# Four groups of the second layer's modulation run at the end of the first layer's experts instead of inside its attention stage

## The chip, the cores and the metric

The program runs on one core of one Trainium2 chip. The metric is the device time of one execution in microseconds (us). The core's engines are PE (TensorE matmuls), PEld (its weight loads), DVE (VectorE), ACT (ScalarE), POOL (GpSimd) and SP (SyncE, which here issues almost all DMAs); each runs its own instructions in order and waits on semaphores for the others. A name such as L297 is a line of the kernel.

## The reference

Two layers of a diffusion transformer over 512 latent and 256 context tokens of width 1024, in f32. What matters here, cut from the reference:

```
m_lat = split(c_act @ w_mod[layer] + b_mod[layer], 6)          # w_mod[layer]: 1024 x 6144
m_ctx = split(c_ctx_act @ w_mod[layer] + b_mod[layer], 6)
h  = rmsnorm(x,  norm1_g[layer]) * (1 + m_lat[1]) + m_lat[0]
hc = rmsnorm(xc, norm1_g[layer]) * (1 + m_ctx[1]) + m_ctx[0]
p = h @ w_in[layer];  pc = hc @ w_in[layer]                     # then four mixers, one of them MLA, one HGRN
x = x + m_lat[2] * (concat(mixers) @ w_out[layer])
h2 = rmsnorm(x, norm2_g[layer]) * (1 + m_lat[4]) + m_lat[3]
x = x + m_lat[5] * hierarchical_moe(h2)                         # 32 experts, top 2 of one group
```

In the first layer the context tokens go through the same steps. The modulation is a product with two rows (c_act and c_ctx_act), but a matrix of 24 MB for each layer. It depends on c and c_ctx alone, not on the tokens.

## The kernel before

**Modulation.** `modulation(L, gs, slot, bank)` (L322) works in groups of 512 of the 6144 columns. For a group it loads the bias (two small DMAs, L332) into one of four tiles `bmt` and the weights in two DMAs of 1 MB (L337), does 64 matmuls whose two useful rows come from `cT` (L338), adds the bias on DVE (`mr`, L341) and, for groups 0 to 3, transposes (L343) and copies the result into `ABs[L]` (L344, L349). Groups 0 to 3 are m[0] and m[1]: they are what `htmp`, the modulated tokens at the very start of a layer (L505), needs. `drain` runs a generator to its end; `weave` runs several side by side, each with a number of steps.

**Stages of a layer.** Norm and projection w_in with the first mixer's work; GLA and neighbourhood attention; then the stage that matters here, in which HGRN, MLA and `mods()` (L1431) are woven (L1436, `STEPS[L][6]` to `[8]`); then the output projection, the routing and the experts. In the first layer `mods()` does groups 4 to 11 of this layer and behind them groups 0 to 3 of the next. In the second layer it does groups 4 to 11 alone.

**Experts.** Their weights (three 1 MB pieces of each of 32) stream through 18 slots (`wslot`), loaded by SP far ahead (`prefetch`). `pair(p_)` is two experts; 16 pairs run one after another, each ending in a scatter of `yes` into `XA` in DRAM by POOL (L2013). A pair may have more tokens than its tile holds, for which there are branches (L2038 and on), and behind the loop stands a branch for what is left over (L2052, `If(cregs[NP] > 64)`). It isn't taken with these inputs. At its untaken side every engine passes an unconditional branch with waits.

**Start of the next layer.** `fetch` loads 128 tokens from `XA` (`xn<-XA`, L473); ACT squares and sums (`junk`, L481), and `rstd_of` takes Ln (L300) and Exp (L301); DVE scales `xn` (L487); PE transposes it (L498); ACT makes `htmp` (L505). `wchunk` loads a piece of w_in (L522), which ACT and DVE split into two parts (L527, L531): the first piece is small (128 columns), and behind its split, which a call `fixed` ties in the order, comes a load of an activation table that holds both Ln and Exp (`ln_exp`, L191). A scheduler orders the instructions of each engine by costs and dependences; an activation that needs a table that isn't in place gets a load of its own.

Of the kernel before, what the change touches and what calls it, by code (L numbers as in the profile page):

```python
# [17 lines left out]
P = 128  # L18
# [7 lines left out]
NEXP = 32  # L26
# [7 lines left out]
YE = 3  # L34
PRE = 2

STEPS = ((38, 24, 60, 18, 12, 12, 66, 72, 12), (38, 24, 60, 18, 12, 12, 66, 72, 8))
NWM = 4
NU, NX, NM = 25, 8, 8
TOKS = ((256, 512), (0, 256))  # L40
# [45 lines left out]
def hybrid_kernel(ctx: ExitStack, tc: tile.TileContext, a: dict, out: bass.AP, dbg=None, stop=None):  # L86
    nc = tc.nc
# [235 lines left out]
    for t_ in bmt:  # L323
        V.memset(t_, 0.0)

    def modulation(L, gs, slot=None, bank=None):

        for i_, g in enumerate(gs):
            cs = slice(g * 512, (g + 1) * 512)
            bt = bmt[i_ % 4]  # L330
            for w in range(2):
                nc.sync.dma_start(bt.rearrange("(j r) c -> j r c", r=32)[:, w, :], a["b_mod"][L, cs].rearrange("(j c) -> j c", j=4))  # L332
            pm = bank()[:, 0:P] if bank else pmd()
            for k in range(KT):
                if k % 4 == 0:
                    wt = (slot or ring)([P, 4, 512])
                    nc.sync.dma_start(wt, a["w_mod"][L, k * P:(k + 4) * P, cs].rearrange("(k p) c -> p k c", p=P))  # L337
                for j in range(4):  # L338
                    mm(pm[32 * j:32 * j + 32, 0:P], cT[:, k, :], wt[:, k % 4, j * P:(j + 1) * P], k == 0, k == KT - 1)
            mr = cp.tile([P, P], F32, name="mr", tag="mr", bufs=2)  # L340
            V.tensor_tensor(mr, pm[:, 0:P], bt, op=ALU.add)  # L341
            if g < 4:
                TE.transpose(pm[:, 0:P], mr, ident)  # L343
                V.tensor_copy(ABs[L][:, :, g // 2, 4 * (g % 2):4 * (g % 2) + 4],  # L344
                              pm[:, 0:P].rearrange("p (j c) -> p c j", j=4)[:, 0:2, :])
            if g in (2, 3):
                ks = slice(4 * g - 8, 4 * g - 4)
                for w in range(2):
                    V.scalar_tensor_tensor(ABs[L][:, w, 1, ks], ABs[L][:, w, 1, ks], 1.0, g1s[:, L, ks], op0=ALU.add, op1=ALU.mult)  # L349
            if g in (8, 9):  # L350
                g2 = cp.tile([P, P], F32, name="g2", tag="g2", bufs=1)
                V.memset(g2, 0.0)
                for w in range(2):
                    nc.sync.dma_start(g2.rearrange("(j r) c -> j r c", r=32)[:, w, :],
                                      a["norm2_g"][L, (g - 8) * 512:(g - 7) * 512].rearrange("(j c) -> j c", j=4))
                V.scalar_tensor_tensor(mr, mr, 1.0, g2, op0=ALU.add, op1=ALU.mult)
            if 6 <= g < 10:
                TE.transpose(pm[:, 0:P], mr, ident)
                V.tensor_copy(AB2s[L][:, :, g // 2 - 3, 4 * (g % 2):4 * (g % 2) + 4],
                              pm[:, 0:P].rearrange("p (j c) -> p c j", j=4)[:, 0:2, :])  # L360
            if g >= 4:
                if g in (6, 7):

                    V.tensor_copy(bt.rearrange("p (e q) -> p q e", e=2), mr.rearrange("p (q e) -> p q e", e=2))
                for w in range(2):
                    if g in (6, 7):
                        nc.sync.dma_start(MOD[L][w, 3 * D:4 * D].rearrange("(e i j q) -> i j e q", e=2, i=2, j=4)[g - 6],
                                          bt.rearrange("(j r) (e q) -> j r e q", r=32, e=2)[:, w])
                    else:
                        nc.sync.dma_start(MOD[L][w, cs].rearrange("(j c) -> j c", j=4),  # L370
                                          mr.rearrange("(j r) c -> j r c", r=32)[:, w, :])
            yield
# [18 lines left out]
    def layer(L):  # L391
        last = L == DEPTH - 1
# [1037 lines left out]

        def mods():  # L1431
            yield from modulation(L, range(4, 12))
            if not last:
                yield from modulation(L + 1, range(4))

        weave((hgrn_, st[6]),  # L1436
              (chain(mla_qkv(Em, hu, cs, c2, mw, mr_), restore(Ex), mla(Em, mr_)), st[7]), (mods(), st[8]))
# [15 lines left out]
        def wslot():  # L1453
            i = pieces[0] % NW
            pieces[0] += 1
            for p_, n_ in slots:
                if i < n_:
                    return wpools[p_].tile([P, 2048], F32, name=f"w{p_}", tag=f"w{p_}", bufs=n_)
                i -= n_
# [21 lines left out]
        def prefetch(n, order=True, after=None, deep=DEEP):  # L1481

            for _ in range(n):
                e, i = len(loaded) // 6 + NEXP // 2 * (len(loaded) % 2), len(loaded) % 6 // 2
                if len(loaded) < 3 * NEXP:
                    loaded.append(expert_part(wgu[e], wdn[e], i, order, after, deep))
# [432 lines left out]
        def block_in(xg, xT=None, engs=(S.copy, V.tensor_copy)):  # L1919
# [8 lines left out]
                engs[g](xT[:, 4 * g:4 * g + 4], pt.rearrange("p (k t) -> p k t", k=4))  # L1928
            return xT

        def span(hv):
            return slice(64 * hv[0], 64 * hv[-1] + 64)

# [33 lines left out]
        def gates_of(own):  # L1967

            if last:
                return gate[:, 0]  # L1970
            gt = gts[:, 0]
            G.tensor_scalar(gt, gate[:, 1], own, None, op0=ALU.mult)
            G.tensor_tensor(gt, gt, gate[:, 0], op=ALU.add)
            return gt
# [35 lines left out]
        def scatter(ye, row):  # L2010


            G.indirect_dma_start(out=XA, out_offset=bass.IndirectOffsetOnAxis(ap=row, axis=0), in_=ye, in_offset=None,  # L2013
                                 bounds_check=T - 1, oob_is_err=False, compute_op=ALU.add)
# [3 lines left out]
        def pair(p_):  # L2018
            return [loaded[6 * p_ + h:6 * p_ + 6:2] for h in range(2)] if p_ >= 0 else None
# [5 lines left out]
        xT = block_in(xgs[0], None, (S.copy, S.copy))  # L2025
        for p_ in range(NP):
            prefetch(max(0, min(6 * p_ + NW, 3 * NEXP) - len(loaded)), False)
            w_ = pair(p_)
            xT_, ac = xT, block_up(w_, xT)
            if p_ == 0:  # L2030
                slot_weights(ohs, tabs[0])
                slot_weights(slot_table(wk, 1, tabs[1]["row"]), tabs[1])
            rows(p_ + NG)
            if p_ + 1 < NP:
                xT = into(p_ + 1)
            gt = gates_of(tab(0, p_, "own"))
            ye = weighted(p_, block_down(w_, block_act(ac)), gt, tab(0, p_, "gws"))
            with tc.If(cregs[p_] > 0):  # L2038
                with tc.If(cregs[p_] < 2) as c1_:
                    half_swapped(p_, w_[0], xT_, ye, gt, 1)  # L2040
                with c1_.Else():
                    with tc.If(cregs[p_] < 3) as c2_:
                        half_swapped(p_, w_[1], xT_, ye, gt, 0)
                    with c2_.Else():
                        swapped(p_, w_, xT_, ye, gt)

                        gather(yes[:, (p_ + 2) % YE], tab(1, p_, "row"))
                        y1 = block_down(w_, block_act(block_up(w_, into(p_, 1, xT_))))
                        scatter(weighted(p_ + 1, y1, gates_of(tab(1, p_, "own")), tab(1, p_, "gws")), tab(1, p_, "row"))
            scatter(ye, tab(0, p_, "row"))  # L2050

        with tc.If(cregs[NP] > 64):  # L2052
            for b in range(2, 12):
                t_ = tables(wk, "g")
                slot_weights(slot_table(wk, b, t_["row"]), t_)
                for i_, n_ in enumerate(kinds):
                    nc.sync.dma_start(TBL[:, :, (b - 2) * nk + i_].rearrange("a p -> p a"),
                                      t_[n_] if n_ == "row" else t_[n_].bitcast(I32))
            pieces[0] = 6
            with tc.For_i(0, NP) as e:  # L2060
                w_ = [[expert_part(wgu[bass.ds(e + NP * h, 1)].rearrange("o k c -> (o k) c"),
                                   wdn[bass.ds(e + NP * h, 1)].rearrange("o k c -> (o k) c"), i) for i in range(3)]
                      for h in range(2)]
                ix = wk.tile([P, 10 * nk], I32, name="ix", tag="ix", bufs=2)
                nc.sync.dma_start(ix, TBL[bass.ds(e, 1)].rearrange("o p b -> (o p) b")[:, 0:10 * nk])
                for b in range(10):
                    g_ = {n_: ix[:, nk * b + i:nk * b + i + 1] if n_ == "row" else ix[:, nk * b + i:nk * b + i + 1].bitcast(F32)
                          for i, n_ in enumerate(kinds)}
                    gather(xgs[b % 2], g_["row"])
                    y1 = block_down(w_, block_act(block_up(w_, block_in(xgs[b % 2]))))  # L2070
                    scatter(weighted(b, y1, gates_of(g_.get("own")), g_["gws"]), g_["row"])
        ec.close()
        ed.close()
        ew.close()
# [66 lines left out]
```

## Time and profile before

| | before |
|---|---|
| three runs | 1742.36, 1739.35, 1741.66 us (median 1741.66) |
| profiled execution | 1741.17 us, span 1739.4 us |
| mean granted TensorE clock | 0.938 |
| PE, PEld busy | 1447.7 us (83%), 985.1 us (57%) |
| DVE, ACT, POOL busy | 700.0 us (40%), 536.6 us (31%), 338.8 us (19%) |
| DMA | 366.01 MB, mean 210 GB/s |

Busy time is a mean over stages with different limits, so the stages are read apart. The first layer's woven stage lies about at 340 to 508 us, its experts at 606 to 915 us, the second layer's start at 922 us, and its woven stage at about 1204 to 1352 us.

### The profile page before, as it was taken

How to read it: one execution, taken by the hardware profiler on the slowest of the kernel's cores; microseconds unless marked ns; L12 is line 12 of the kernel's file. 1: busy time of each engine (PE TensorE's matmuls, PEld its weight loads, DVE VectorE, ACT ScalarE, POOL GpSimd, SP SyncE). 2: the span in 40 equal slices, each digit the busy share in tenths (PEclk: the TensorE clock that was granted, in tenths of full speed). 3: DMA queues.
4: the chain of work that ended last, by engine and by line, in shares of the span. 5: the costliest groups of instructions: out<-in, count | busy, mean ns of one | idle time of the engine just before them, and what ended most of it. 6: DMA issues, size and time to landing. Idle time of an engine off the chain costs nothing. (4 is left out here: it accounts for less than half of the span.)

```text
span 1739.4 us, 26685 instructions
## 1 busy us (share of the span) xinstructions
PE 1447.7 (83%) x10515; PEld 985.1 (57%) x10515; DVE 700.0 (40%) x1415; ACT 536.6 (31%) x1086; POOL 338.8 (19%) x262
## 2 busy tenths in 40 slices
PE   6999999989889848887885989999787775887883
PEld 4888778746669823322234978677366672332221
DVE  5263353477733452211114452635876244111111
ACT  5342453464422220100004442624743121100001
POOL 0022121120102233554430020301111122111100
PEclk9999989999999969999997999989898897999997
DMA  9332411057548599999985332211533598999996
GB/s 319 95 117 69 125 57 34 33 190 245 174 149 230 164 385 327 382 373 386 372 297 144 98 89 72 75 31 56 165 127 119 190 308 328 381 347 368 379 382 236
DMA packets 179833, 366.01 MB, mean 210 GB/s; under 512 B 39673, under 2 KB 90529, under 8 KB 179361
## 3 DMA queue, kind: packets, MB, share of 16 engines
q1 hardware_dynamic: 167440, 335.54, 54.7%
q0 software_dynamic: 9216, 20.99, 4.8%
q10 hardware_dynamic: 2960, 6.58, 1.0%
q8 instruction: 138, 2.26, 0.5%
q14 instruction: 79, 0.64, 0.1%
HBM read 338.48 MB, written 39.65 MB: 217 GB/s over the span
## 5 line engine op out<-in xcount | busy, mean ns | idle before, releaser
L297 PE MATMUL mm<-w,xT 128*64 128x512 f32 (+1 forms) x1120 | 269.5, 591 | 31.8 <-DMA w<-in_moe_w_gu_dram 13.3
L297 PE MATMUL pj<-h,w 128*128 128x256 f32 (+1 forms) x1224 | 228.2, 342 | 0.5 <-DVE u L945 0.3
L297 PEld LDWEIGHTS pj<-h,w 128*128 128x128 f32 x1224 | 190.0, 192 | 28.7 <-issue 5.2
L297 PEld LDWEIGHTS mm<-w,xT 128*64 128x64 f32 x1120 | 89.2, 139 | 188.0 <-issue 138.5
L297 PE MATMUL sc<-w,aT 128*64 128x512 f32 x536 | 131.5, 600 | 19.5 <-ACT aT L1953 16.5
L297 PE MATMUL pj<-w,h 128*128 128x256 f32 x864 | 118.3, 294 | 0.0
L297 PEld LDWEIGHTS pj<-w,h 128*128 128x128 f32 x864 | 111.4, 199 | 3.8 <-issue 3.1
L2013 POOL DMA_INDIRECT XA<-yes,row x32 | 50.9, 1590 | 305.3 <-DVEq L2038 254.1
L1943 ACT ACTIVATE ac<-mm 128x256 f32<-128x256 f32 x32 | 12.3, 383 | 312.0 <-PE mm L297 312.0
L1944 DVE TENSOR_TENSOR ac<-ac,mm 128x256 f32<-128x256 f32 x32 | 13.5, 421 | 226.2 <-ACT ac L1943 226.2
L297 PE MATMUL mm<-w,h 128*128 128x256 f32 x624 | 84.2, 296 | 14.0 <-PEq L1526 6.4
L531 DVE TENSOR_TENSOR w<-w 128x2048 fp32r<-128x2048 f32 (+1 forms) x26 | 58.0, 2230 | 91.3 <-ACT w L527 91.3
L297 PEld LDWEIGHTS sc<-w,aT 128*64 128x64 f32 x536 | 42.3, 136 | 85.7 <-issue 54.7
L297 PEld LDWEIGHTS mm<-w,h 128*128 128x128 f32 x624 | 80.8, 203 | 14.7 <-issue 6.6
L1624 POOL TENSOR_TENSOR xh<-xc,gr 128x512 f32<-128x512 f32 (+1 forms) x25 | 30.2, 1208 | 194.2 <-DVE xc L1620 89.7
L297 PE MATMUL sc<-h 128*128 128x256 f32 (+3 forms) x144 | 60.2, 535 | 8.8 <-ACT um L1221 7.8
L1927 PEld LDWEIGHTS pt<-masks,xgr 128*128 128x128 f32 x256 | 28.8, 147 | 68.1 <-issue 68.1
L1927 PE MATMUL pt<-masks,xgr 128*128 128x128 f32 x256 | 40.7, 293 | 31.5 <-DMA xgr<-XG,row 18.0
L527 ACT ACTIVATE w<-w 128x2048 fp32r<-128x2048 f32 (+1 forms) x26 | 48.0, 1847 | 60.6 <-PE pj L297 36.8
L297 PE MATMUL x<-u 64*32 64x32 f32 (+5 forms) x944 | 54.0, 251 | 12.0 <-DVE u L785 9.6
L297 PE MATMUL sc<-h,w 128*128 128x512 f32 (+1 forms) x312 | 59.4, 350 | 0.3 <-ACT ux L300 0.3
L297 PEld LDWEIGHTS x<-u 64*64 64x64 f32 (+4 forms) x944 | 45.4, 146 | 24.3 <-issue 9.1
(399 smaller groups left out, 2367.8 us busy)
## 6 DMA issues: line engine op xcount, KB each, us to landing
w<-in_moe_w_gu_dram SPq DMA_DIRECT2D x128, 1024.0 KB
w<-in_moe_w_dn_dram SPq DMA_DIRECT2D x64, 1024.0 KB
w<-in_w_mod_dram SPq DMA_DIRECT2D x40, 1024.0 KB
w<-in_w_in_dram SPq DMA_DIRECT2D x22, 1024.0 KB
wm<-in_w_mod_dram SPq DMA_DIRECT2D x8, 1024.0 KB
XG<-xh ACTq DMA_DIRECT2D x10, 512.0 KB
w<-in_w_out_dram SPq DMA_DIRECT2D x8, 512.0 KB
w<-in_w_out_dram SPq DMA_DIRECT2D x16, 256.0 KB
```

The lines of the kernel that those rows point to most:

```text
L297: TE.matmul(o, lhsT, rhs, start=start, stop=stop, **kw)
L527: sp = S.activation(hi[:, :, 0:o], raw[:, :, 0:o], AF.Copy)
L531: V.tensor_tensor(lo[:, :, 0:o], raw[:, :, 0:o], hi[:, :, 0:o].bitcast(F32), op=ALU.subtract)
L1624: G.tensor_tensor(xh[:, t0 - qt0:t0 - qt0 + m].rearrange("p n (e c q) -> p c n q e", e=2, c=4)[:, c], xs.rearrange(pairs, e=2), bc(gr[:, 1 ...
L1927: TE.transpose(pt[:, u * P:(u + 1) * P], xg[:, o:o + P], ident)
L1943: S.activation(ac[rs_], pm[rs_, 0:256], AF.Silu)
L1944: V.tensor_tensor(ac[rs_], ac[rs_], pm[rs_, 256:512], op=ALU.mult)
L2013: G.indirect_dma_start(out=XA, out_offset=bass.IndirectOffsetOnAxis(ap=row, axis=0), in_=ye, in_offset=None, bounds_check=T - 1, oob_is_er ...
```

## The change

Groups 0 to 3 of the second layer leave the first layer's `mods()`; its step number goes from 12 to 8, as in the second layer. Their bias and weights now go into expert slots that have come free: behind the last expert's loads, at the 15th and 16th pair, `mod_ahead` takes one slot for the biases (cleared by a DVE memset of 128x512, then 8 small DMAs) and eight slots for the weights (8 DMAs of 1 MB). The 256 matmuls and what follows them run behind the leftovers' branch, in the order of the code. The slot numbers that the branch's own weights use move up behind them.

```
-STEPS = ((38, 24, 60, 18, 12, 12, 66, 72, 12), (38, 24, 60, 18, 12, 12, 66, 72, 8))
+STEPS = ((38, 24, 60, 18, 12, 12, 66, 72, 8), (38, 24, 60, 18, 12, 12, 66, 72, 8))
...
+    def mod_bias(L, g, bt):
+        for w in range(2):
+            nc.sync.dma_start(bt.rearrange("(j r) c -> j r c", r=32)[:, w, :],
+                              a["b_mod"][L, g * 512:(g + 1) * 512].rearrange("(j c) -> j c", j=4))
+
+    def mod_weights(L, g, kh, wt):
+        nc.sync.dma_start(wt, a["w_mod"][L, kh * 512:(kh + 1) * 512, g * 512:(g + 1) * 512].rearrange("(k p) c -> p k c", p=P))
+
+    def modulation(L, gs, slot=None, bank=None, there=None):
...
-            bt = bmt[i_ % 4]
-            for w in range(2):
-                nc.sync.dma_start(bt.rearrange("(j r) c -> j r c", r=32)[:, w, :], a["b_mod"][L, cs].rearrange("(j c) -> j c", j=4))
+            bt = there[g][2] if there else bmt[i_ % 4]
+            if not there:
+                mod_bias(L, g, bt)
...
-                    wt = (slot or ring)([P, 4, 512])
-                    nc.sync.dma_start(wt, a["w_mod"][L, k * P:(k + 4) * P, cs].rearrange("(k p) c -> p k c", p=P))
+                    if there:
+                        wt = there[g][k // 4]
+                    else:
+                        wt = (slot or ring)([P, 4, 512])
+                        mod_weights(L, g, k // 4, wt)
...
         def mods():
             yield from modulation(L, range(4, 12))
-            if not last:
-                yield from modulation(L + 1, range(4))
...
+        ahead = {}
+
+        def mod_ahead(g):
+            if not ahead:
+                bs = wslot()
+                V.memset(bs[:, 0:512], 0.0)
+                for g_ in range(4):
+                    ahead[g_] = [None, None, bs[:, g_ * P:(g_ + 1) * P]]
+                    mod_bias(L + 1, g_, ahead[g_][2])
+            for kh in range(2):
+                ahead[g][kh] = wslot().rearrange("p (k c) -> p k c", k=4)
+                mod_weights(L + 1, g, kh, ahead[g][kh])
...
         for p_ in range(NP):
             prefetch(max(0, min(6 * p_ + NW, 3 * NEXP) - len(loaded)), False)
+            for g in () if last else range(4):
+                if 6 * p_ + NW >= 3 * NEXP + 2 * g + 3 and (not ahead or ahead[g][0] is None):
+                    mod_ahead(g)
...
-            pieces[0] = 6
+            pieces[0] = 6 if last else 3 * NEXP + 9
...
+        if not last:
+            drain(modulation(L + 1, range(4), None, pmm, ahead))
         ec.close()
```

Three places of the built programs show what moves. Line numbers in rows of the changed kernel are its own: L328 and L332 are there the loads of a bias and of modulation weights, L484 that of `xn` and L533 that of a piece of w_in, L492 `junk`, L516 `htmp`, L538 the split on ACT, and L2078 the leftovers' branch.

The first place is SP behind the last expert's load and the branches of the last pair, in the changed kernel. Ahead of these rows, between the last loads, stand the eight bias loads (`w_15464<-in_b_mod_dram`) and the first two weight loads.

```order
L332 DMA w_15480<-in_w_mod_dram 128x4x512 [waits DMAHW4_49]
L332 DMA w_15703<-in_w_mod_dram 128x4x512 [waits DMAHW5_49]
L332 DMA w_15705<-in_w_mod_dram 128x4x512 [waits DMAHW6_49,PE_49]
L332 DMA w_15707<-in_w_mod_dram 128x4x512 [waits DMAHW7_49]
L332 DMA w_15709<-in_w_mod_dram 128x4x512 [waits DMAHW0_49,PE_49]
L2078 COMPARE_AND_BRANCH
```

Before, no load stands between the last expert's and the leftovers' compare (L2052). Now eight loads of 1 MB do, the last of them right ahead of the compare (L2078).

The second place is SP at the start of the second layer: first before, from the branch at the untaken side of L2052.

```order
L2052 UNCONDITIONAL_BRANCH [waits DMAHW0_49,DMAHW1_49,DMAHW2_49,DMAHW3_49,DMAHW4_49,DMAHW5_49,DMAHW6_49,DMAHW7_49]
L522 DMA w<-in_w_in_dram 128x8x64 [waits DMASW4_49,DMASW5_49,DMASW0_49,DMASW7_49,DVE_49,DMAHW1_49,PE_49,Pool_49]
L522 DMA w<-in_w_in_dram 128x8x32 [waits DMAHW2_49]
L522 DMA w<-in_w_in_dram 128x8x32 [waits DMAHW3_49]
L473 DMA xn_17222<-XA 128x1024 [waits DMAHW4_49,DMASW3_49]
L473 DMA xn_17229<-XA 128x1024 [waits DMAHW5_49]
L522 DMA w<-in_w_in_dram 128x8x256 [waits DMAHW6_49]
L473 DMA xn_17237<-XA 128x1024 [waits DMAHW7_49]
```

The same place in the changed kernel:

```order
L2078 UNCONDITIONAL_BRANCH [waits DMAHW0_49,DMAHW1_49,DMAHW2_49,DMAHW3_49,DMAHW4_49,DMAHW5_49,DMAHW6_49,DMAHW7_49]
L484 DMA xn_17224<-XA 128x1024 [waits DMAHW1_49,DMASW7_49,DMAHW2_49,DMASW3_49,PE_49]
L484 DMA xn_17231<-XA 128x1024 [waits DMAHW3_49,PE_49]
L484 DMA xn_17239<-XA 128x1024 [waits DMAHW4_49,PE_49]
L484 DMA xn_17247<-XA 128x1024
L484 DMA xn_17355<-XA 128x1024 [waits DMAHW5_49]
L533 DMA w<-in_w_in_dram 128x8x64 [waits DMASW5_49,DMASW4_49,DMASW7_49,DMASW0_49,DMAHW6_49,DVE_49,Pool_49]
L533 DMA w<-in_w_in_dram 128x8x32 [waits DMAHW7_49]
```

The branch waits for all eight lanes of SP's DMAs (DMAHW0 to 7) in both. Behind it the small first piece of w_in (64, 32 and 32 columns) came ahead of `xn`; now five `xn` loads come ahead of it.

The third place is ACT at the start of the second layer: first before, from the same branch.

```order
L2052 UNCONDITIONAL_BRANCH
L527 ACTIVATE w<-w 128x8x128
L191 ACT_TABLE_LOAD
L481 ACTIVATE junk,ss<-xn_17222 128x1024
L300 ACTIVATE ss<-ss,eps 128x1
L481 ACTIVATE junk,ss<-xn_17229 128x1024
L301 ACTIVATE ss<-ss 128x1
L300 ACTIVATE ss<-ss,eps 128x1
L301 ACTIVATE ss<-ss 128x1
L527 ACTIVATE w<-w 128x2048
L481 ACTIVATE junk,ss<-xn_17237 128x1024
L505 ACTIVATE htmp<-mm,AB_150 128x256
```

The same place in the changed kernel:

```order
L2078 UNCONDITIONAL_BRANCH
L492 ACTIVATE junk,ss<-xn_17224 128x1024
L300 ACT_TABLE_LOAD
L300 ACTIVATE ss<-ss,eps 128x1
L492 ACTIVATE junk,ss<-xn_17231 128x1024
L301 ACT_TABLE_LOAD
L301 ACTIVATE ss<-ss 128x1
L300 ACT_TABLE_LOAD
L300 ACTIVATE ss<-ss,eps 128x1
L492 ACTIVATE junk,ss<-xn_17239 128x1024
L301 ACT_TABLE_LOAD
L301 ACTIVATE ss<-ss 128x1
```

Before, the split of the first piece of w_in (L527) and the one table load behind it (L191) came first, and Ln and Exp found their table. Now the split (L538) and its table load stand some 20 rows behind the branch, and ahead of them stand seven table loads, one wherever Ln follows Exp or Exp follows Ln.

## Rows read from the trace of the kernel before

**Rows 1.** Busy time of each engine (instructions), TensorE clock, DMA share, GB/s, in four stretches

```profile
340.00:508.00 168.00, 149.47 (x1823) 103.88 (x1824) 113.09 (x228) 81.96 (x178) 25.91 (x20) 0.96 0.54 178
420.00:430.00 10.00, 9.99 (x135) 7.73 (x127) 4.58 (x12) 3.25 (x8) 0.00 (x0) 1.00 0.77 264
450.00:460.00 10.00, 6.52 (x103) 4.27 (x99) 10.00 (x20) 2.25 (x5) 0.09 (x1) 1.00 0.85 268
1204.00:1352.00 148.00, 117.56 (x1338) 81.93 (x1341) 106.19 (x189) 76.64 (x150) 25.30 (x17) 0.92 0.42 139
```

**Rows 2.** Instructions by line, PE, 340 to 508 us: busy, mean ns | idle before

```profile
L297 PE MATMUL x<-w,cT 128*32 128x128 f32 x768 | 27.1, 287 | 2.8 <-DMA w<-in_w_mod_dram 2.2 <-DVE um L1001 0.6
```

**Rows 3.** Timeline of PE in the stage (start, duration, instruction)

```profile
481.77 1.95 PE L297 MATMUL x<-w,cT 128*32 128x128 f32 x64
...
484.41 0.33 PE L343 MATMUL x<-masks,mr 128*128 128x128 f32 x1
```

**Rows 4.** Waits of SP's queue, 890 to 935 us: total, times, longest

```profile
SPq L522 <- remote: 15.5, 1, 15.5
SPq L2052 <- SPq L2052: 9.4, 1, 9.4
```

**Rows 5.** Timeline of SP, 895 to 934 us

```profile
895.98 0.37 SPq L1470 DMA_DIRECT2D w<-in_moe_w_dn_dram  x1
922.43 1.78 SPq L522 DMA_DIRECT2D w<-in_w_in_dram  x3
924.32 1.27 SPq L473 DMA_DIRECT2D xn<-XA  x2
```

**Rows 6.** Stretches, columns as in group 1: the experts and the boundary

```profile
606.00:902.00 296.00, 225.24 (x1085) 90.87 (x1086) 72.68 (x186) 31.16 (x69) 123.41 (x71) 0.93 1.00 370
905.00:915.00 10.00, 7.78 (x36) 2.52 (x32) 2.01 (x4) 0.76 (x2) 6.85 (x3) 1.00 0.36 57
915.00:925.00 10.00, 0.00 (x0) 0.00 (x0) 0.30 (x2) 0.00 (x0) 1.58 (x1) 0.70 0.45 75
925.00:935.00 10.00, 1.56 (x8) 1.48 (x8) 2.64 (x3) 6.24 (x11) 0.00 (x0) 0.50 1.12 333
945.00:955.00 10.00, 9.91 (x83) 9.51 (x82) 5.95 (x18) 5.09 (x13) 0.00 (x0) 1.00 0.01 2
```

**Rows 7.** Timeline of POOL, 905 to 925 us

```profile
915.36 1.58 POOL L2013 DMA_INDIRECT XA<-yes,row  x1 [3.04 <-DVEq L2038]
```

**Rows 8.** Timeline of ACT, the second layer's start

```profile
927.39 1.06 ACT L527 ACTIVATE w<-w 128x1024 fp32r<-128x1024 f32 x1 [16.91 <-DMA w<-in_w_in_dram]
928.46 1.28 ACT L191 ACT_TABLE_LOAD   x1
929.90 1.06 ACT L481 ACTIVATE junk<-xn 128x1024 f32<-128x1024 f32 x1 [0.16 <-DMA xn<-XA]
...
931.09 0.29 ACT L300 ACTIVATE ss<-ss,eps 128x1 f32<-128x1 f32 x1
...
932.33 0.19 ACT L301 ACTIVATE ss<-ss 128x1 f32<-128x1 f32 x1
...
934.11 1.91 ACT L527 ACTIVATE w<-w 128x2048 fp32r<-128x2048 f32 x1 [1.13 <-DMA w<-in_w_in_dram]
...
940.08 2.21 ACT L505 ACTIVATE htmp<-mm,AB 128x256 f32<-128x256 f32 x4
```

**Rows 9.** Timeline of PE, the second layer's start

```profile
939.90 7.05 PE L297 MATMUL pj<-h,w 128*128 128x256 f32 x46
946.79 1.56 PE L498 MATMUL mm<-masks,xn 128*128 128x128 f32 x10
```

**Rows 10.** Timeline of DVE, the second layer's start

```profile
936.05 2.29 DVE L531 TENSOR_TENSOR w<-w 128x2048 fp32r<-128x2048 f32 x1 [2.10 <-ACT w L527]
```

**Rows 11.** Timeline of ACT, the program's start

```profile
4.48 1.28 ACT L260 ACT_TABLE_LOAD   x1 [4.48 <-DMA crow<-in_c_ctx_dram]
5.78 0.31 ACT L260 ACTIVATE crow<-crow 16x128 f32<-16x128 f32 x1
```

More of the change, by code (lines that the diff above doesn't have):

```diff
@@ L324, in hybrid_kernel @@
         V.memset(t_, 0.0)
-    def modulation(L, gs, slot=None, bank=None):
+    def mod_bias(L, g, bt):
[5 more added lines that the diff above has]
+    def modulation(L, gs, slot=None, bank=None, there=None):
         for i_, g in enumerate(gs):
             cs = slice(g * 512, (g + 1) * 512)
-            bt = bmt[i_ % 4]
-            for w in range(2):
-                nc.sync.dma_start(bt.rearrange("(j r) c -> j r c", r=32)[:, w, :], a["b_mod"][L, cs].rearrange("(j c) -> j c", j=4))
+            bt = there[g][2] if there else bmt[i_ % 4]
+            if not there:
+                mod_bias(L, g, bt)
             pm = bank()[:, 0:P] if bank else pmd()
```

## The prediction

> **What bounds the kernel now.** I read the table by stages first, since busy shares over the whole span hide the limits. In the first layer's woven stage, 340 to 508 us, PE is busy 149.47 of 168 us; it is full at 420 to 430 us (9.99 of 10), while at 450 to 460 DVE is full and PE has 6.52 [rows 1]. So this stage changes its limit from PE to DVE and back, with PE the more frequent one. DMA, at a share of 0.54, is not its limit. The experts are bound by DMA: a share of 1.00 at 370 GB/s over 606 to 902 us [rows 6].
>
> Then I read the waits of SP's queue and its timeline, for the boundary between the layers. The last expert load is issued at 895.98; SP then waits 9.4 us in the leftovers' branch, to about 906, when the expert weights have landed, and another 15.5 us for another engine, to 922.43, where it issues the second layer's first loads [rows 4, 5]. The last scatter is issued at 915.36 [rows 7], so the second wait is for the scatter's landing and the other engines' way through the branch. From 915 to 925 PE does nothing and DMA has a share of 0.45; from 925 to 935 PE has 1.56 us [rows 6]. ACT takes up the first tokens at 929.90 [rows 8], and from 945 on PE is full (9.91 of 10) [rows 6]. The boundary is thus one chain: SP's gate, the loads, ACT's statistics and `htmp`, the projection. What is added to it is added to the time.
>
> **The change part by part.** *Removed from the woven stage*: 256 matmuls, four transposes, a few DVE operations and 8.39 MB of loads. In the trace 64 such matmuls in a row take 1.95 us, and the transpose behind them 0.33 [rows 3]; by the mean of all 768, 27.1 us for twelve groups, one group is 2.26 us [rows 2]. Four groups are so 4 x (1.95 + 0.33) = 9.1 us of PE. PE is busy for 89% of the stage (149.47 of 168), which would leave 8.1 us; but where DVE is full nothing is gained, and eight groups are now spread by the weave over the length on which twelve lay. I take two thirds of the 9.1: **6 us**. Bounds: 0, if DVE or a chain sets the stage after all, and 20, the difference to the second layer's stage with its eight groups (148 against 168 us [rows 1]), which lacks the context's part as well, so that 20 is far too much. Nothing behind the stage swallows the gain: the projection and routing follow on PE, and the experts' loads start when their slots come free, so the whole of it moves up.
>
> *Unchanged*: expert loads. The bias and weight loads stand behind them on SP. The memset of 128x512 waits for a slot that pair 13 has left, and DVE has 72.68 of 296 us in the experts' stage [rows 6]: free, and were it not, under 1 us.
>
> *Added, the gate*: the order of SP shows eight 1 MB loads between the last expert load and the branch, and the branch waits for all of SP's DMA lanes. SP can issue nothing for the second layer before these have landed. The expert weights land at about 906. The eight bias loads add some 1.5 us (an estimate: the last of them is held by the last expert's lane), and 8.39 MB at 370 GB/s [rows 6] are 22.7 us: 930. The two last scatters move in that time too; now they take 3.6 us of the DMA engines at 905 to 915 (share 0.36) and about 2 to 3 of the 4.5 at 915 to 925, the rest being the new layer's first loads [rows 6]. The 370 GB/s hold such scatters already, so counting them in full gives an upper bound of 937; near it, since two fall into 25 us, where the experts' stage has one in about 18 (16 pairs in 296 us): **935**, which is 12.6 later than 922.43. Bounds: 930 and 938.
>
> The 256 matmuls follow the weights as they land, four groups by 2.28 us beside 22.7 us of loads; only the last group, some 3 us with its DVE steps, lies behind the last landing, and it is done before the first `htmp`, which needs the tokens to have been loaded and scaled.
>
> *Loads at the gate*: before, three pieces of w_in are issued at 922.43 and then `xn` at 924.32, and ACT starts on `xn` at 929.90, 7.5 us behind the gate [rows 5, 8]. Now `xn` comes first: the 1.9 us of issue and about 0.6 us of transfer are gone, so X, the start of ACT's first square, is 5 us behind the gate: **-2.5**.
>
> *Added, activation tables*: this is the part that the diff does not say. The order of ACT shows seven more table loads at the start of the second layer, since the split of the first piece of w_in, to which the load of the common table is tied, now comes behind. One load takes 1.28 us [rows 8, 11]. In before, the first split (1.06) and the one load ran at 927.39 to 929.74, under the wait for `xn` [rows 8]. Now I count ACT in its order from X to the end of the second split, after which the second piece's matmuls can start: 8 loads of 1.28 (10.3), 6 squares of 1.15 (929.90 to 931.09, less their overlap: 6.9), 10 Ln and Exp of 0.2 (2.0), 10 `htmp` of 0.53 (four take 2.21; 5.3), two splits of 1.06 and 1.91, a copy of 0.3: 27.8. DVE's half of the split adds 2.29 [rows 10]: X + 30.1. In before the second piece's matmuls begin 24 of 48 into the run that starts at 939.90 (two stand ahead of it, 22 x 0.153 us behind its start): 943.3, X + 13.4 [rows 8, 9]. That is **+16.6**. Of it 9.0 are the loads and 2.3 the split and load that had been hidden; the rest is order, since two more squares and two `htmp` now come ahead of that split. In return ten transposes (1.56 us) and a few pairs, which came behind these matmuls, lie ahead of them on an idle PE: **-1.8**. PE is full from there on, so the whole delay is kept.
>
> Is 1.28 all? At the program's start a load at 4.48 ends at 5.76 and the activation behind it starts at 5.78 [rows 11]: no more than its own time.
>
> The Trainium skill (ScalarE: Activation LUTs, What ACT_TABLE_LOAD costs) gives 1283 ns, as here, and a drain of some 1380 ns besides. With that drain seven loads would cost 9.7 us more, and the sum below would be 28.6. The same page (Table sets: the hidden batching unit) has functions loaded as sets, so that Ln and Exp in turn cost nothing only under a set that holds both; this speaks against the change, and the row orders agree with it.
>
> **Sum**: -6 + 12.6 - 2.5 + 16.6 - 1.8 = +18.9. The profiled execution took 1741.17, so 1760.1; it stands 0.5 below the median of the runs shown, so 1760.
>
> **The rivals.** *Hidden loads* (B): the loads cost nothing because ACT would wait anyhow, for `xn` pieces at 512 KB each or for PE's transposes. For it: before, ACT waits 1.13 us at 934.11 and has slack until 929.90 [rows 8]. Against it: `xn` comes at more than 300 GB/s (333 at 925 to 935 [rows 6]), one in 1.6 us, while ACT needs over 3 for each. It gives 9.0 less, 1751; with the gate at 930 as well, 1746.
>
> *The drain* (C): each load holds ACT 1.38 us longer than the rows show. Against it the gap of 0.02 us [rows 11]; for it, that only one load of the few there was followed by work that was ready. It gives 1770.
>
> *Other side* (D): the woven stage's length hangs on its modulation groups by far more than their PE time, since each group makes PE wait for a weight DMA (2.2 us of waits in twelve groups [rows 2]) and holds PE, DVE and PE again in turn. It then shrinks to the second layer's 148 us [rows 1]: a gain of 20 against 24.9 for the boundary, 1746. It decides from 24.9 on, or from 19.9 with the gate at its lower bound of 930; there it is no longer slower, 1741 to 1742. Against it: 2.2 us of waits are all that could come on top of 9.1.
>
> That the change doesn't do what it says is excluded by the orders: the matmuls do stand behind the branch.
>
> **How the numbers follow.** The forecast (with the gate between 930 and 938, and 0 to 9 from the stage: 1752 to 1768) has 0.70, B 0.14, C 0.11, D 0.05. The range reaches down through B to 1746 and up to C at 1770, and leaves out about 0.15. A measurement of this kernel can tell 0.2%, 3.5 us, from no change. Faster than 1738 needs D and a cheap boundary: 0.03. Within 1738 to 1745 lie D's main part and the bottom of B: 0.05. Slower: 0.92.
>
> **What would show it.** In the profile after: (1) the woven stage ends 4 to 9 us earlier, and so do the experts; (2) SP's first load of the second layer comes some 29 us behind the last expert weight's landing, in place of 16.5, with DMA full until shortly ahead of it; (3) ACT has eight table loads in the first 22 us behind the first `xn`, each 1.28 us with the next activation right behind it; (4) the second piece's projection starts about 30 us behind ACT's first square, and PE is idle in between for more than half of the time; (5) from there to the end every stage has its old length. The prediction is wrong if SP gets through the branch before the modulation weights have landed, if the table loads lie under a wait that ends later, or if the woven stage loses 15 us or more.

## The result, and the profile after

The changed kernel took 1761.37 us (median of five runs, 1752.5 to 1764.38) against 1741.66 before: 1.0103 times as long, 95% interval 1.0081 to 1.0125. The profiled execution is the shortest of the five, 1752.5 us with a span of 1750.5; the other four lie between 1759.9 and 1764.4. Its rows are read first, and what the others have besides comes with the first experiment.

Five points of time carry the comparison: the end of the first layer's experts on PE (the end of their last matmul), the gate (SP's first load for the second layer), X (ACT's first square there), the start of the run of 144 projection matmuls from which PE is full in both kernels, and the end of the span.

| us | experts' end | gate | X | 144 matmuls | span |
|---|---|---|---|---|---|
| before | 914.2 | 922.4 | 929.9 | 969.2 | 1739.4 |
| after | 904.1 | 924.2 | 928.7 | 981.3 | 1750.5 |
| difference of the step | -10.2 | +12.0 | -3.0 | +13.4 | -1.1 |

The last row is each step's own: the woven stage and all behind it up to the experts' end give 10.2, then the gate lies 20.2 behind them in place of 8.2, X 4.5 behind the gate in place of 7.5, and the chain behind X, up to the 144 matmuls, takes 52.7 in place of 39.3. Their sum is the 11.1 by which the span grew.

SP in the changed kernel, the answer to [rows 5]:

```profile
879.93 2.91 SPq L1479 DMA_DIRECT2D w<-in_moe_w_dn_dram  x2
882.88 10.21 SPq L328 DMA_DIRECT2D w<-in_b_mod_dram  x8
893.19 17.53 SPq L332 DMA_DIRECT2D w<-in_w_mod_dram  x8
924.23 3.43 SPq L484 DMA_DIRECT2D xn<-XA  x5
927.91 5.55 SPq L533 DMA_DIRECT2D w<-in_w_in_dram  x3
```

SP is through with the last two expert loads 2.91 us behind 879.93, 13.5 earlier than before. Then the eight bias loads take SP 10.2 us, and only at 893.19 the first of the eight weight loads goes out. Of the 10.2, 5.9 are three waits for experts' loads that are still landing (total, times, longest):

```profile
SPq L328 <- DMA w<-in_moe_w_dn_dram: 4.0, 2, 2.0
SPq L328 <- DMA w<-in_moe_w_gu_dram: 1.9, 1, 1.9
```

The gate opens at 924.23. SP's wait in the branch is 12.7 us now, and the long wait for another engine of [rows 4] is gone. Stretches of 5 us show what the DMA engines did meanwhile (last two columns: DMA share, GB/s):

```profile
885.00:890.00 5.00, 3.26 (x28) 2.32 (x26) 0.42 (x1) 0.64 (x2) 0.00 (x0) 1.00 0.75 302
890.00:895.00 5.00, 5.00 (x26) 1.72 (x24) 2.65 (x3) 0.58 (x1) 0.00 (x0) 1.00 0.17 29
895.00:900.00 5.00, 3.90 (x20) 1.07 (x15) 0.42 (x1) 0.45 (x2) 4.70 (x3) 1.00 1.02 374
900.00:905.00 5.00, 3.70 (x16) 1.31 (x16) 1.50 (x2) 0.30 (x1) 2.15 (x1) 1.00 1.05 292
905.00:910.00 5.00, 0.00 (x0) 0.00 (x0) 0.00 (x0) 0.00 (x0) 1.58 (x1) 0.81 1.05 393
910.00:915.00 5.00, 1.01 (x20) 1.04 (x24) 0.00 (x0) 0.00 (x0) 0.00 (x0) 0.50 1.05 308
915.00:920.00 5.00, 5.00 (x106) 4.30 (x101) 0.46 (x2) 0.00 (x0) 0.00 (x0) 0.67 1.04 391
920.00:925.00 5.00, 4.66 (x144) 3.85 (x138) 1.15 (x6) 0.00 (x0) 0.00 (x0) 1.00 0.29 107
```

While the bias loads wait, the share falls to 0.17. From 895 on it is 1.02 to 1.05, at 292 to 393 GB/s, and it falls shortly ahead of the gate. By these rows it is the eight weight loads that the gate waits for; the runs of the boundary alone, with and without them, test it.

ACT from X on, the answer to [rows 8], and PE beside it, the answer to [rows 9]:

```profile
928.68 1.06 ACT L492 ACTIVATE junk<-xn 128x1024 f32<-128x1024 f32 x1 [28.37 <-DMA xn<-XA]
...
929.84 1.28 ACT L300 ACT_TABLE_LOAD   x1
931.14 0.30 ACT L300 ACTIVATE ss<-ss,eps 128x1 f32<-128x1 f32 x1
931.34 1.04 ACT L492 ACTIVATE junk<-xn 128x1024 f32<-128x1024 f32 x1
...
932.49 1.28 ACT L301 ACT_TABLE_LOAD   x1
933.78 0.20 ACT L301 ACTIVATE ss<-ss 128x1 f32<-128x1 f32 x1
934.00 1.28 ACT L300 ACT_TABLE_LOAD   x1
...
947.06 1.04 ACT L538 ACTIVATE w<-w 128x1024 fp32r<-128x1024 f32 x1
948.12 1.28 ACT L191 ACT_TABLE_LOAD   x1
...
954.95 1.92 ACT L538 ACTIVATE w<-w 128x2048 fp32r<-128x2048 f32 x1
```

```profile
900.36 3.70 PE L297 MATMUL sc<-w,aT 128*64 128x512 f32 x16 [0.52 <-ACT aT L1976]
913.99 4.44 PE L297 MATMUL mm<-w,cT 128*32 128x128 f32 x74 [9.94 <-PEq L2078]
...
935.76 1.11 PE L509 MATMUL mm<-masks,xn 128*128 128x128 f32 x4 [0.26 <-DVE AB L355]
...
956.92 0.74 PE L297 MATMUL pj<-h,w 128*128 128x256 f32 x4 [1.36 <-ACT w L538]
...
959.24 10.81 PE L297 MATMUL pj<-h,w 128*128 128x256 f32 x88 [0.17 <-DVE w L542]
...
981.33 17.44 PE L297 MATMUL pj<-w,h 128*128 128x256 f32 x144
```

Between squares, Ln and Exp stands one table load after another. Three of the groups of table loads in the whole program, by line (count | total, mean ns | idle before):

```profile
L300 ACT ACT_TABLE_LOAD x4 | 5.1, 1283 | 0.1
...
L191 ACT ACT_TABLE_LOAD x3 | 3.8, 1283 | 0.1
L301 ACT ACT_TABLE_LOAD x3 | 3.8, 1283 | 0.1
```

L191 has three in the whole program, as before; the four of L300 and the three of L301 are new. Each takes 1.28 us, and the activation behind it starts about 0.02 later (929.84, 931.14). From X to the start of the second piece's long run of matmuls, ACT is busy for 28.93 of 30.56 us and PE for 14.50:

```profile
928.68:959.24 30.56, 14.50 (x67) 10.44 (x67) 14.16 (x33) 28.93 (x49) 0.00 (x0) 0.61 0.40 118
```

The second split ends at 956.87, X + 28.2; PE starts the second piece's matmuls at 956.92 and runs on from 959.24, X + 30.6, when DVE's half is there.

### The profile page after: what moved, and what is told of

Same layout as the page of the kernel before. It is cut to its first block, busy times and chain, and to the rows that moved or that the text cites. A ratio compares the mean times of both kernels' runs of the same rounds, so it can differ in the third digit from the quotient of the medians.

```text
span 1750.5 us, 26685 instructions
## 1 busy us (share of the span) xinstructions
PE 1451.1 (83%) x10515; PEld 984.8 (56%) x10515; DVE 702.1 (40%) x1416; ACT 545.9 (31%) x1093; POOL 340.6 (19%) x262
## 5 line engine op out<-in xcount | busy, mean ns | idle before, releaser
L297 PE MATMUL sc<-w,aT 128*64 128x512 f32 x536 | 135.8, 600 | 20.1 <-ACT aT L1976 17.0
L1967 DVE TENSOR_TENSOR ac<-ac,mm 128x256 f32<-128x256 f32 x32 | 13.5, 420 | 226.1 <-ACT ac L1966 226.1
L1633 POOL TENSOR_TENSOR xh<-xc,gr 128x512 f32<-128x512 f32 (+1 forms) x25 | 30.2, 1209 | 191.8 <-DVE xc L1629 77.4
L538 ACT ACTIVATE w<-w 128x2048 fp32r<-128x2048 f32 (+1 forms) x26 | 48.0, 1846 | 43.9 <-PE pj L297 37.8
L1937 ACT COPY xT<-pt 128x512 f32<-128x512 f32 x34 | 19.9, 586 | 129.1 <-PE pt L1936 122.0
```

What stands on the lines that cost most here:

```text
L297: TE.matmul(o, lhsT, rhs, start=start, stop=stop, **kw)
L538: sp = S.activation(hi[:, :, 0:o], raw[:, :, 0:o], AF.Copy)
L1633: G.tensor_tensor(xh[:, t0 - qt0:t0 - qt0 + m].rearrange("p n (e c q) -> p c n q e", e=2, c=4)[:, c], xs.rearrange(pairs, e=2), bc(gr[:, 1 ...
L1967: V.tensor_tensor(ac[rs_], ac[rs_], pm[rs_, 256:512], op=ALU.mult)
```

## The experiments

Their medians stand beside those of the kernel before on the same chip (1741.6 to 1743.1); where a time is set against another's points, these were read in its trace as above.

**The changed kernel again**, unaltered.

> The changed kernel once more, unaltered. Its profiled run of 1752.5 us is the shortest of five, the others took 1760 to 1764 at a lower mean clock (0.929 against 0.936). My theory has +20 us at the boundary between the layers (gate and table loads) in every run, and what differs between its runs is the gain of the woven stage and the stages behind it up to the experts: a run of about 1761 then shows a granted clock below the profiled one's somewhere between 340 and 610 us and the experts ending 8 to 9 us later, with the boundary unchanged to 1 us. Rival: the landing of the modulation weights varies, so that the gate itself comes 8 to 9 us later behind the last expert weight. Time by both: 1752 to 1764.

Measured: 1761.3 us, 1.0103 (1.0078 to 1.0128); this time the profiled execution is a long one, span 1758.9, 8.4 over the other. Its points: experts' end 907.5, gate 927.4, X 931.9, the 144 matmuls 984.9. So gate, X and chain have the same lengths to 0.4 us (19.9, 4.5, 53.1); 3.5 us come up to the experts' end and 4.8 behind the boundary. The second layer's routing starts at 1448.90 and 1457.23, and from there the two are equal to 0.1 us. Between lies the second layer's woven stage, here in the shorter and then in the longer execution, each from its first `sc<-ux,ones` matmul to the first half of its last modulation group (after the DVE, ACT and POOL columns: clock, DMA share, GB/s):

```profile
1205.80:1360.44 154.64, 119.94 (x1323) 82.84 (x1321) 108.73 (x193) 79.97 (x157) 25.32 (x17) 0.96 0.41 135
```

```profile
1207.13:1368.84 161.71, 131.75 (x1324) 89.13 (x1322) 109.26 (x193) 80.02 (x157) 24.93 (x17) 0.87 0.40 129
```

The mean granted clock is 0.96 in one and 0.87 in the other, and the stage is 7.1 us longer; 2.3 of these had been won between the 144 matmuls and the stage. The stage's instructions are not touched by the change. Over all thirteen profiles its length goes with its clock: 154.6 to 154.7 us at 0.96 (two profiles), 156.6 to 156.9 at 0.92 to 0.93 (five, the kernel before among them), 159.0 at 0.90 (one), 161.5 to 161.7 at 0.87 (five). The rival, a gate that varies, falls; my place for it, between 340 and 610 us, was right for 1.1 of 8.4 (the first layer's routing starts at 603.6 and 604.7), and 2.4 more came within the first layer's experts.

**A power on POOL in place of Ln and Exp**, in the second layer's first norm; SP's order at the boundary is the changed kernel's.

```
-                rstd_of(ss, ss, D)
+                if L:
+                    rstd_col(ss, D)
+                else:
+                    rstd_of(ss, ss, D)
```

> The second layer's first norm takes its reciprocal root with a power on POOL in place of Ln and Exp on ACT, and nothing else: five of the seven added table loads have no cause left, nor the other two; ACT's order and SP's order at the boundary stay those of the changed kernel. Also 10 Ln and Exp of 0.2 us leave ACT. Theory (ACT's loads are on the chain): 9 to 11 us below the changed kernel in the same state, 1750 where that is 1761. Rival (the loads lie under the waits for the tokens or for the second piece of w_in): within 3 us of the changed kernel.

Measured: 1749.34 us, 1.0040 (1.0020 to 1.0060), 12 below the changed kernel. ACT there:

```profile
932.98 1.06 ACT L492 ACTIVATE junk<-xn 128x1024 f32<-128x1024 f32 x1 [27.55 <-DMA xn<-XA]
...
934.17 1.06 ACT L492 ACTIVATE junk<-xn 128x1024 f32<-128x1024 f32 x1
...
943.65 1.04 ACT L541 ACTIVATE w<-w 128x1024 fp32r<-128x1024 f32 x1
944.72 1.28 ACT L191 ACT_TABLE_LOAD   x1
...
951.67 1.90 ACT L541 ACTIVATE w<-w 128x2048 fp32r<-128x2048 f32 x1
```

The squares follow each other and one table load is left at the boundary. The gate, 20.0 behind the experts, is as in the changed kernel, X lies 3.8 behind the gate (4.5 there), and the chain behind X takes 43.3 in place of 52.7 to 53.1: 9.3 to 9.7 less. So the table loads were on the chain. The same edit to the kernel before is the control:

> Control for the run with the power on POOL: the same edit made to the kernel before, whose boundary has one table load, hidden. Only the 10 Ln and Exp of 0.2 us leave ACT there. Theory (what the edit won in the changed kernel was the table loads): 0 to 2 us below before, 1739.5 to 1742. Rival (the edit wins by itself, with no regard to table loads): 6 us or more below before.

Measured: 0.9996 (0.9972 to 1.0020); the medians differ by more, 1739.26 against 1743.09, and two of the twelve runs took 1753 and 1755. Its chain is 38.8, where before has 39.3. By itself the edit is worth 0.5 us of chain. Between 38.8 and the 43.3 above lie 4.5 us that are not the seven loads, since neither run has them. What is left is the order, w_in behind the tokens: the first split and its one table load, 2.3 us, now come behind X as well.

**Two groups ahead instead of four.**

```
-STEPS = ((38, 24, 60, 18, 12, 12, 66, 72, 8), ...
+STEPS = ((38, 24, 60, 18, 12, 12, 66, 72, 10), ...
             yield from modulation(L, range(4, 12))
+            if not last:
+                yield from modulation(L + 1, range(2))
...
-            drain(modulation(L + 1, range(4), None, pmm, ahead))
+            drain(modulation(L + 1, range(2, 4), None, pmm, ahead))
```

> Only groups 2 and 3 are moved to the experts' end; groups 0 and 1 stay in the woven stage (its step number is 10). Four loads of 1 MB instead of eight stand behind the last expert load, and in the built order the first piece of w_in comes ahead of the tokens again, so that only one table load is left. Theory: the modulation weights land at some 920 on the clock of before, ahead of the scatter's landing, so the gate is where it was, the table loads are gone, and 3 to 7 us of the woven stage are won: 1735 to 1741. Rival (the transfer itself is the whole loss, at half the bytes half of it): 1750.

Measured: 1740.14 us, 0.9986 (0.9966 to 1.0007). SP:

```profile
886.60 2.92 SPq L1481 DMA_DIRECT2D w<-in_moe_w_dn_dram  x2
889.56 2.25 SPq L328 DMA_DIRECT2D w<-in_b_mod_dram  x4
891.92 7.68 SPq L332 DMA_DIRECT2D w<-in_w_mod_dram  x4
917.18 1.80 SPq L533 DMA_DIRECT2D w<-in_w_in_dram  x3
919.09 1.22 SPq L484 DMA_DIRECT2D xn<-XA  x2
```

The gate is 9.3 behind the experts' end (8.2 before) and the chain 37.2 (39.3 before): the boundary costs nothing any more (55.4 us from PE's end to the 144 matmuls, 54.9 before). The experts end at 907.9.

**Without the weight loads**, the matmuls reading the last experts' weights.

```
-                ahead[g][kh] = wslot().rearrange("p (k c) -> p k c", k=4)
-                mod_weights(L + 1, g, kh, ahead[g][kh])
+                ahead[g][kh] = loaded[-3 - kh]
```

> The eight loads of modulation weights are left out, and the 256 matmuls read the last experts' weights in their place (so the second layer's first modulation is not the reference's); biases are still loaded. In the built order only one table load is left at the boundary. Theory: the gate stands as before or up to 2 us later, the matmuls lie on an idle PE, and the woven stage's gain remains whole: 6 to 10 us below before, 1731 to 1736. Rival (what costs is the way through the branch, the waits on the slots and the 256 matmuls behind it, not the weights' transfer): 1745 or more.

Measured: 1764.13 us, against 1731 to 1736. Both theories miss why: the second layer's modulation is another, so its router is given other values. The trace has 26984 instructions for 26685, and from the start of the second routing to the end the span takes 323.9 us where the other profiles take 299 to 303. Up to there it is a fair run: gate 8.8 behind the experts' end, the 144 matmuls at 968.4. The whole time says nothing, so the question was put again with the first four groups computed rightly as well.

**The boundary alone, with and without its loads.** The woven stage does all twelve groups at the old step number, and the change's end of the experts is made besides, into a tile that is not read.

```
             yield from modulation(L, range(4, 12))
+            if not last:
+                yield from modulation(L + 1, range(4))
...
+        AB_ = ABx if there else ABs[L]
```

> Groups 0 to 3 stay in the woven stage as in the kernel before (step number 12), and the changed kernel's whole addition at the end of the experts is made besides, its result going to a tile that nobody reads. The built order at the boundary is the changed kernel's, with its seven added table loads and the tokens' loads ahead of w_in. So the price of the boundary is there without the gain of the stage. Theory: the woven stage and the experts end as before, the boundary is 22 to 25 us longer: 1763 to 1767 against a median of 1741.6. Rival (the change's loss lies in the stages behind or in the clock, not at the boundary): below 1755.

> As boundary_only, but without the eight weight loads: the 256 matmuls read the last experts' weights, and the result goes to a tile that nobody reads, so the output is the reference's. In the built order w_in comes ahead of the tokens and one table load is left. This mends the run without weights, whose second layer was routed otherwise. Theory: without the transfer the gate stands where it was; the tokens' loads wait for the 256 matmuls, which cost up to 5 us: 1742 to 1747. Rival (the branch, the bias loads and the matmuls are the price): 1755 or more.

Measured: 1770.26 us, 1.0173 (1.0145 to 1.0201), with the loads, and 1748.85 us, 1.0045 (1.0024 to 1.0065), without. SP with the loads, and without:

```profile
891.01 2.93 SPq L1484 DMA_DIRECT2D w<-in_moe_w_dn_dram  x2
893.98 10.24 SPq L330 DMA_DIRECT2D w<-in_b_mod_dram  x8
904.32 18.83 SPq L334 DMA_DIRECT2D w<-in_w_mod_dram  x8
935.20 2.38 SPq L487 DMA_DIRECT2D xn<-XA  x5
```

```profile
894.32 10.24 SPq L330 DMA_DIRECT2D w<-in_b_mod_dram  x8
921.37 3.72 SPq L536 DMA_DIRECT2D w<-in_w_in_dram  x4
925.20 11.42 SPq L487 DMA_DIRECT2D xn<-XA  x6
```

With them the gate is 23.4 behind the experts' end and the chain 53.1; without, 8.4 and 39.2 (with one table load), and X is 10.8 behind the gate, since the tokens' loads now wait for the 256 matmuls (six loads in 11.42 us). Both were 2 to 3 us above what I had expected at most. For the first, the boundary is 25.3 longer than before, and 3.7 more came behind it, at a clock of 0.87 in the second layer's woven stage. That the price lies at the boundary, and there on the transfer and what comes with it, holds. The two runs differ in the order at the boundary too (w_in first again without the loads), so this pair alone doesn't tell the transfer from the order; the power's run and the next one do.

The 23.4 in place of 20.2 are not a longer transfer. Counted from the end of SP's issue of the last expert load, the gate comes 41.3 to 41.6 us later in all five profiles with eight loads behind late biases (the changed kernel twice, the power, this run, the old step number below), and 26.1 later before: 15.2 to 15.5 more. PE's end of the experts lies 21.2 to 21.8 behind that load in the changed kernel and with the power, and 17.8 to 17.9 in the other two and before. So it is the loads that set the gate, and the distance from PE's end changes with what PE has left to do behind the last load.

**Biases loaded ahead of the expert loop**, into the tiles `bmt`; all four groups moved.

```
-                bs = wslot()
-                V.memset(bs[:, 0:512], 0.0)
                 for g_ in range(4):
-                    ahead[g_] = [None, None, bs[:, g_ * P:(g_ + 1) * P]]
-                    mod_bias(L + 1, g_, ahead[g_][2])
+                    ahead[g_] = [None, None, bmt[g_]]
...
+        for g_ in () if last else range(4):
+            mod_bias(L + 1, g_, bmt[g_])
         xT = block_in(xgs[0], None, (S.copy, S.copy))
```

> All four groups are moved as in the change, but their biases are loaded into the four bias tiles ahead of the expert loop, so that SP issues the first weight load right behind the last expert load. In the profile of the changed kernel the eight bias loads cost SP 10.2 us there, each waiting for a lane, and the DMA share falls to 0.17 at 890 to 895 us. In the built order w_in comes ahead of the tokens again and one table load is left. Theory: the gate comes 5 to 7 us earlier than in the changed kernel, X lies 7.5 us behind it in place of 4.5, and the chain behind X is that of before (13 us shorter): about 15 us below the changed kernel, 1743 to 1748. Rival (eight loads can't be hidden, whatever their order; only the tables go): 1750 or more.

Measured: 1744.21 us, 1.0018 (1.0004 to 1.0033), 17 below the changed kernel. The stretches of the hole:

```profile
885.00:890.00 5.00, 3.55 (x17) 1.51 (x18) 0.52 (x2) 0.76 (x2) 0.00 (x0) 1.00 0.99 384
890.00:895.00 5.00, 4.16 (x36) 3.10 (x32) 1.68 (x3) 0.38 (x1) 0.00 (x0) 1.00 0.98 384
895.00:900.00 5.00, 4.10 (x12) 1.37 (x14) 0.14 (x1) 0.65 (x2) 0.00 (x0) 0.66 1.05 398
```

SP there:

```profile
890.48 23.56 SPq L332 DMA_DIRECT2D w<-in_w_mod_dram  x8
923.94 4.45 SPq L533 DMA_DIRECT2D w<-in_w_in_dram  x3
```

The hole is gone (0.98 in place of 0.17 at 890 to 895). The gate comes 33.5 behind SP's last expert load, where the changed kernel has 41.4 and before 26.1. So about half of what the gate had grown by came with the eight small loads and their slot, and not with the 8.39 MB. X lies 9.5 behind the gate, since w_in comes first again (4.5 in the changed kernel), which takes 5.0 of these 7.9 back, and the chain is 40.7 with one table load, 12.0 to 12.4 less. How much of this is the table loads isn't told apart by this run alone; the power's run gives 9.3 to 9.7 for them.

**The old step number** (8 to 12 in the changed kernel), nothing else.

> The changed kernel with the modulation's step number at 12 again, so that its eight groups run at the old pace and end at two thirds of the woven stage. The boundary is the changed kernel's, with its seven table loads. Theory (PE's sum of work is what the stage loses, not the pace): within 3 us of the changed kernel, 1758 to 1764. Rival (the pace decides what the stage gains): 5 us or more off.

Measured: 1763.81 us, 1.0124 (1.0100 to 1.0148): 2.5 above the changed kernel, within what was expected. The pace is not what the gain hangs on, as far as the time tells; what differs inside is told under the gain below.

**Candidates for a better kernel**: two groups with the power, and two groups with early biases (the edits above, joined).

> Two groups ahead, and the second layer's first norm by a power on POOL, so that Ln and Exp are gone from ACT's chain at the boundary. Theory: the gate as with two groups ahead, ACT's chain shorter by up to 2 us: 1737 to 1740, 1 to 4 below before. Rival: POOL's steps take on the chain what ACT's give: as with two groups ahead, 1740.

> Groups 2 and 3 ahead, with their biases loaded ahead of the expert loop into two of the bias tiles. The four weight loads follow the last expert load directly and land ahead of the scatter; one table load at the boundary. Theory: the boundary is that of before, and what the experts pass on of the two groups' PE time is won, 2 to 4 us: 1737 to 1740. Rival (the experts' stage, bound by DMA, takes it back): 1740 to 1743.

Measured: 1740.18 us, 0.9990 (0.9970 to 1.0009), and 1740.94 us, 0.9993 (0.9977 to 1.0009). Chains 39.1 and 37.5, gates 9.2 behind the experts' end in both. No version is shown to be faster than the kernel before; each takes back what the change lost.

## Why the prediction was right

Forecast were 1760 and a loss at the boundary; 1761.4 came, and the loss lies there. The mechanism holds. That the sum is met to 1.4 us is in part luck, since terms that were off by up to 3 us cancel. Term by term:

- **The gain of the woven stage** (forecast 6): 10.2 at the experts' end in the profile after, 6.7 in the second one. One profile of before is a poor base, though: in four profiles with twelve groups in that stage the experts end at 911.4 to 914.2 (mean 912.6), in the six with eight groups at 904.1 to 912.3 (mean 908.7): 3.9. The first layer's routing starts at 612.3 to 618.1 and at 603.6 to 610.4, means 614.5 and 607.1: 7.4, or 1.9 for a group, close to the 1.95 + 0.33 of [rows 3]. So the stage gives nearly all of its PE time, and on PE the experts' stage keeps about half. I had written that nothing behind the stage swallows the gain; for PE that step was wrong. What is seen: in the changed kernel PE waits 4.0 us for an expert's weights near 872, which it doesn't before, and the granted clock is 0.56 for 870 to 875. All five profiles with eight groups at step number 8 have this wait, and from the routing to the experts' end they take 300.4 to 304.1 us; the sixth, with the old step number, hasn't and takes 299.4. The four with twelve groups take 296.1 to 299.1, one of them with a wait of 3.9 us as well. So the wait is not the whole loss, and its cause remains open. The gate of the changed kernel hangs on the loads, however, and these kept more: SP's last expert load goes out 6.7 us earlier in the mean (887.8 for 894.5), close to the forecast 6. The medians of the boundary alone with its loads and of the changed kernel differ by 1770.3 - 1761.3 = 9.0, which is not the gain alone, since the boundary itself, from PE's end to the 144 matmuls, takes 80.3 in the one and 77.3 to 77.4 in the other.
- **The gate** (forecast +12.6): +12.0 from PE's end, and 11.7 in the second execution; but from the last expert load, on which it hangs, +15.2 to 15.5, so the term was some 2.7 too small. I had allowed 1.5 us for the bias loads; the DMA engines had a hole of some 5 us there, and with early biases the gate comes 7.9 sooner behind that load. The weights' transfer I had priced too high: without the late biases the gate is 33.5 behind the last expert load, where my 935 less the 1.5 makes 37. Counting from 895 to the fall of the share, 8.39 MB took 26.5 us, 317 GB/s.
- **Loads at the gate** (-2.5): -3.0.
- **The chain on ACT** (+16.6 - 1.8 = +14.8): +13.4, and 13.8 in the second execution. Counted X + 30.1 for the second piece, measured X + 30.6. The seven loads are real, and the power on POOL takes 9.3 to 9.7 off with them (9.0 and part of 2.0 for Ln and Exp).
- **The table loads' price**: 1.28, with about 0.02 ahead of it and behind it in every one, so the rival of a longer hold (1770) falls. The rival of hidden loads (1751 or 1746) falls by the power on POOL; and the shrinking stage (a gain of 20), since six profiles with eight groups give 7.4 at the routing. The Trainium skill (ScalarE: Activation LUTs, What ACT_TABLE_LOAD costs) has 1283 ns, which agrees, and a drain of about 1380 ns on top, which these rows do not show.
- **The rest**: unchanged in the profiled run (769.2 us from the 144 matmuls, 770.2 before), but 774.0 in the second, by the clock in a stage that the change does not touch. I had no term for that; without these 3.8 us the 1760.9 of the second execution would be 1757. In the profiles of the power on POOL and of the boundary alone, with and without loads, the rest is 773 to 774 too; in the one without loads the woven stage is not the longer one (156.7 us at 0.92). What sets the clock wasn't found.

## What to carry to other kernels

Work that moves to a point where an engine idles brings its transfers with it: 8 MB that were free in a stage with a DMA share of 0.54 stood behind a DMA-bound stage and ahead of a branch that waits for every lane. Look at the built order, not at the diff alone: of the 22 us by which the boundary grew, 9.3 to 9.7 came from a scheduler that turned two groups of loads around, so that a table load tied to one of them came too late and seven others took its place. Small loads between large ones count as well: eight of 2 KB held the gate back by up to 7.9 us. And move only as much as the idle time at the new place holds; two groups were free there, four cost 22 us.

## What the runs showed of the hardware that was not expected

Eight small loads of 2 KB held SP for 10.2 us, 5.9 of it in waits for 1 MB loads that were still landing, and the DMA share fell to 0.17 for 5 us. The mean granted clock of one stage with the same instructions was 0.96 in one execution and 0.87 in another of the same kernel, and the stage took 154.6 and 161.7 us.
